# A column gain behind the transposes, and a column stage in written order

## The chip, the cores and the metric

The kernel runs on one core of a Trainium2 chip. The core has a matrix engine (PE), a vector engine (DVE), an activation engine (ACT), a general engine (POOL) and a sync engine (SP), each with its own queue of instructions, and DMA queues that move data between main memory and the on-chip buffers. [...] The metric is the device time of one execution in microseconds. Lower is better.

## The reference

Two layers of a hybrid block over 256 tokens of width 1024, in float32. Each layer normalises x, projects it to 8960 columns, runs four mixers on parts of them (retention A, a gated convolution B, spatial gating C, sliding-window attention D), gates and merges them, and ends in a feed-forward part:

```python
h = rms_norm(x, norm1_g)
z = h @ w_in
za, zb, zc, zd, zg = jnp.split(z, IN_SPLITS, axis=-1)
ya = retention(za, ret_gn_g)
yb = conformer_conv(zb, conv_w, conv_b, conv_ln_g, conv_ln_b)
yc = spatial_gating(zc, gmlp_ln_g, gmlp_ln_b, gmlp_ws, gmlp_bs)
yd = swa_attention(zd, swa_q_g, swa_k_g, swa_sinks, rel_bias)
...
x = x + (mix @ w_out).astype(x.dtype)
h = rms_norm(x, norm2_g)
gt, up = jnp.split(h @ w_ffn_in, 2, axis=-1)
return x + ((jax.nn.silu(gt) * up) @ w_ffn_out).astype(x.dtype)
```

`rms_norm` multiplies x by the inverse root of the mean of its squares and by a gain per column. The change touches how this is computed before the first layer, and the order of the work on `z` in both.

## The kernel before

**Tiles and weights.** The 256 tokens are two tiles of 128 (t = 0, 1). All weights come as *units* of 128 x 2048 values in two halves, in the order of `unit_plan`. A half is fetched (`raw`), rounded by ACT to its high part (`wh`, L119), and DVE subtracts to get its low part (`wl`, L120). Eight buffers of each kind hold four units; six hold raw halves. A 512-column product needs two units. The activations are split in the same way into `hT` high and low (`split`: ACT L176, DVE L178/L180), after PE has transposed them in blocks of 128 x 128 (L169). `mm` makes each product from three matmuls: high x high (L142), high x low weight (L143), low x high (L144). PSUM is four banks `acc`, for the long products, and four banks `mid`, for everything short.

**Opening.** x arrives in two 512-column pieces of tile 0, then four weight halves, then tile 1. ACT and DVE sum the squares, POOL raises to the power -0.5 (`rsqrt`, L186), DVE multiplies x by that factor and by the gain (L239). In the opening the gain comes as two rows of 512, and PE spreads it over 128 partitions with a matmul against a column of ones (L293). PE fills the time before its first work with matmuls on a zeroed tile (`warm_up`, L322). POOL also makes a wide copy (L336) of the table of relative positions. Then come the query columns (units 0 and 1) and the key and value columns (unit 2, 256 wide) of tile 0 and tile 1.

**Column stage (`columns`).** Behind these come eight *chunks*, each of two units over both tiles: convolution a, convolution gate, rotary query, rotary key, retention value, retention gate, gMLP v, gMLP u. The small work of the four mixers is written as generators. `chunk` calls `tick` after each unit, which advances every live generator to its next `yield`; so a `yield` is a step of one unit, about 24 long matmuls.

- `swa_task`: squares, sums and power of queries and keys (L383 to L388, L186), scaled queries and keys (L393, L399), a copy of the values by ACT (`sv`, L405); transposes and their copies (L414, L415); scores by PE (L432), maxima on DVE (L439), exponentials on ACT (L453), their scaling on ACT (L459); transposes of the weights (L469), products with the values (L480).
- `conv_task`: the gate's tanh on ACT (`cvth`, L488), which reads the gate's accumulators, the gate on DVE, transposes to `uT`, then 31 taps on DVE (L510).
- `rot_task`: rotation on DVE (L574 to L582), transposes and copies to `rqk` (L725). `ret_task`: the gate, then scores, products and norm of the retention.

**Who orders the work.** Within a block called `manual_schedule` the named engines issue as the program is written. Before the change that holds for the opening alone, on PE, ACT and DVE. Everywhere else a scheduler orders each engine's instructions. DMAs marked with `keep_in_program_order` stay in written order; before, these are x and the first two units. `take` starts the loading of units two ahead of the one in use (`LOOK`).

## Time and profile before

| What | Value |
|---|---|
| Time, median of 3 runs | 963.24 us (963.23 to 963.3) |
| Profiled execution: its own time | 963.76 us |
| Profiled execution: span, first to last instruction | 961.7 us |
| Mean granted clock of PE | 0.995 |
| Busy: PE, PE weight loads, DVE, ACT, POOL | 952.5, 792.4, 709.7, 507.7, 38.3 us |
| Weight fetches | 320 of 512 KB, median 4.1 us to landing |
| Bytes moved by DMA | 177.00 MB, mean 184 GB/s |

All times below are microseconds from the span's start. A row of the timeline shows its start, how long the group runs, the engine, the line and the tiles (written tile, arrow, read tiles), the count, and in brackets the idle time of the engine just before with what released it. The profiled execution's time is 2.1 us over its span, for what lies before the first and behind the last instruction.

### The profile page before, as it was taken

How to read it: one execution, taken by the hardware profiler on the slowest of the kernel's cores; microseconds unless marked ns; L12 is line 12 of the kernel's file. 1: busy time of each engine (PE TensorE's matmuls, PEld its weight loads, DVE VectorE, ACT ScalarE, POOL GpSimd, SP SyncE). 2: the span in 40 equal slices, each digit the busy share in tenths (PEclk: the TensorE clock that was granted, in tenths of full speed). 3: DMA queues.
4: the chain of work that ended last, by engine and by line, in shares of the span. 5: the costliest groups of instructions: out<-in, count | busy, mean ns of one | idle time of the engine just before them, and what ended most of it. 6: DMA issues, size and time to landing. Idle time of an engine off the chain costs nothing.

```text
span 961.7 us, 12735 instructions
## 1 busy us (share of the span) xinstructions
PE 952.5 (99%) x4686; PEld 792.4 (82%) x4686; DVE 709.7 (74%) x1117; ACT 507.7 (53%) x758; POOL 38.3 (4%) x41
## 2 busy tenths in 40 slices
PE   8999999999999999999999999999999999999998
PEld 5877888888888888888888778888888888888886
DVE  6479999996667766566575699999775677666562
ACT  6298555444635655545464864545445555555550
POOL 1200010000100000000010000200010000000000
PEclk7999999999999999999999999999999999999999
DMA  9764736656546656656557155465655357656621
GB/s 335 209 224 157 254 127 224 193 187 208 177 157 197 219 176 199 195 177 183 166 177 239 66 197 178 151 196 182 202 184 177 113 193 244 194 177 197 196 89 44
DMA packets 50125, 177.00 MB, mean 184 GB/s; under 512 B 5613, under 2 KB 7182, under 8 KB 49936
## 3 DMA queue, kind: packets, MB, share of 16 engines
q1 hardware_dynamic: 49824, 176.07, 56.0%
q8 instruction: 37, 0.61, 0.3%
q14 instruction: 24, 0.20, 0.1%
q10 hardware_dynamic: 240, 0.12, 0.0%
HBM read 174.93 MB, written 1.25 MB: 183 GB/s over the span
## 4 chain that ended last, share of the span: by engine, by line
PE 96%; ACT 1%; DVE 1%; DMA 1%; issue 0%; ACTq 0%; POOL 0%; DVEq 0%; POOLq 0%
PE acc L143 22%; PE acc L144 22%; PE acc L142 22%; PE mid L198 14%; PE mid L201 7%; PE mid L169 3%; PE mid L142 2%; PE mid L143 2%; PE mid L144 2%; ACT sc L453 1%; DMA rel<-rel_bias 1%; PE mid L480 1%; PE mid L469 0%; PE mid L652 0%; DVE wl L120 0%; PE mid L600 0%
## 5 line engine op out<-in xcount | busy, mean ns | idle before, releaser
L120 DVE TENSOR_TENSOR wl<-raw,wh 128x1024 fp32r<-128x1024 f32 x318 | 383.3, 1220 | 129.0 <-ACT wh L119 126.5
L119 ACT CAST wh<-raw 128x1024 fp32r<-128x1024 f32 x318 | 330.8, 1052 | 226.5 <-PE acc L144 129.5
L142 PE MATMUL acc<-wh,hT 128*128 128x512 f32 (+1 forms) x640 | 249.2, 390 | 0.0
L143 PE MATMUL acc<-wl,hT 128*128 128x512 f32 (+1 forms) x640 | 247.1, 386 | 0.2 <-DVE wl L120 0.2
L144 PE MATMUL acc<-wh,hT 128*128 128x512 f32 (+1 forms) x640 | 246.9, 386 | 0.0
L198 PE MATMUL mid<-hT,wh 128*128 128x512 f32 x576 | 203.5, 398 | 0.0
L201 PE MATMUL mid<-hT,wl 128*128 128x256 f32 x576 | 161.7, 281 | 0.0
L142 PEld LDWEIGHTS acc<-wh,hT 128*128 128x128 f32 x640 | 120.8, 189 | 25.0 <-ACT hT L176 1.1
L144 PEld LDWEIGHTS acc<-wh,hT 128*128 128x128 f32 x640 | 120.7, 189 | 24.4 <-DVE hT L180 0.6
L143 PEld LDWEIGHTS acc<-wl,hT 128*128 128x128 f32 x640 | 120.9, 189 | 23.8 <-DVE wl L120 0.8
L198 PEld LDWEIGHTS mid<-hT,wh 128*128 128x128 f32 x576 | 108.1, 188 | 26.2
L142 PE MATMUL acc<-wh,yT 128*128 128x512 f32 x304 | 118.9, 391 | 0.0
L144 PE MATMUL acc<-wh,yT 128*128 128x512 f32 x304 | 118.4, 390 | 0.0
L143 PE MATMUL acc<-wl,yT 128*128 128x512 f32 x304 | 118.4, 389 | 0.0
L201 PEld LDWEIGHTS mid<-hT,wl 128*128 128x128 f32 x576 | 108.8, 189 | 0.4
L510 DVE SCALAR_TENSOR_TENSOR ca<-uT,col,ca 128x256 f32<-128x256 f32 x240 | 101.3, 480 | 3.8 <-ACT ca L504 3.7
L144 PEld LDWEIGHTS acc<-wh,yT 128*128 128x128 f32 x304 | 57.1, 188 | 12.0
L142 PEld LDWEIGHTS acc<-wh,yT 128*128 128x128 f32 x304 | 57.1, 188 | 11.9
L143 PEld LDWEIGHTS acc<-wl,yT 128*128 128x128 f32 x304 | 57.1, 188 | 11.5
L806 ACT ACTIVATE gth<-acc 128x512 f32<-128x512 f32 x32 | 19.1, 597 | 31.0 <-PE acc L144 31.0
L186 POOL TENSOR_TENSOR rs<-rs,nhalf 128x1 f32<-128x1 f32 (+1 forms) x12 | 15.5, 1296 | 373.0 <-DVE rs L525 369.9
L840 DVE TENSOR_TENSOR x<-x,acc 128x512 f32<-128x512 f32 x16 | 10.9, 684 | 24.8 <-PE acc L144 24.8
(161 smaller groups left out, 718.8 us busy)
## 6 DMA issues: line engine op xcount, KB each, us to landing
raw<-wu SPq DMA_DIRECT2D x320, 512.0 KB, 4.1
rows<-rows SPq DMA_DIRECT2D x2, 768.0 KB, 8.7
ng<-norms SPq DMA_DIRECT2D x3, 512.0 KB, 4.2
const<-const SPq DMA_DIRECT2D x1, 1088.0 KB
bias<-rd SPq DMA_DIRECT2D x8, 128.0 KB, 6.0
out<-x SPq DMA_DIRECT2D x4, 256.0 KB, 2.0
x<-x SPq DMA_DIRECT2D x2, 256.0 KB, 3.2
x<-x SPq DMA_DIRECT2D x1, 512.0 KB, 7.9
```

The lines of the kernel that those rows point to most:

```text
L119: nc.scalar.copy(h, src)
L120: nc.vector.tensor_tensor(out=lo, in0=src, in1=h.bitcast(F32), op=ALU.subtract)
L142: nc.tensor.matmul(ps, xh, hs, start=start, stop=False)
L143: nc.tensor.matmul(ps, xh, ls, start=False, stop=False)
L144: nc.tensor.matmul(ps, xl, hs, start=False, stop=stop)
L169: self.nc.tensor.transpose(ps[:, b * P : (b + 1) * P], src[:, b * P : (b + 1) * P], self.ident)
L186: self.nc.gpsimd.tensor_tensor(out=out, in0=v, in1=self.nhalf[:, :n], op=ALU.pow)
L198: nc.tensor.matmul(ps.rearrange("p (s t m) -> p s t m", s=2, t=T), h[:, c : c + P], both, start=start, stop=False)
L201: nc.tensor.matmul(ps[:, : T * P].rearrange("p (t m) -> p t m", t=T), lo[:, c : c + P], self.hT[:, :, 0, k, :], start=False, stop=stop,)
L510: nc.vector.scalar_tensor_tensor(out=self.ca[:, c, :], in0=self.uT[:, c, k : k + T * P], scalar=w[:, c, k : k + 1], in1=self.ca[:, c, :], ...
L806: self.nc.scalar.activation(th[t, n], ps[t], AF.Tanh, scale=0.5)
L840: self.nc.vector.tensor_tensor(out=xs, in0=xs, in1=ps, op=ALU.add)
```

## The change

**Opening.** The gain is no longer spread over partitions. It arrives as eight columns beside the identity matrix (`first`), x is scaled by the root alone (tile halves n = 0 on ACT, n = 1 on DVE), PE transposes it, and DVE then multiplies the transposed half, where a column of gain stands on the partitions, while it copies it out of PSUM to `gT` (`gained`). ACT and DVE split `gT` into high and low. The products are issued half by half of the weights (`half`): per half all high x high, then low x high, then high x low weight. Six weight halves instead of four are fetched ahead of tile 1. The warm-up matmuls number 11, 3, 4 and 3 instead of 7, 3, 1 and 1.

**Column stage.** `columns` of both layers stands in a manual block for PE, ACT, DVE and POOL. The retention's value and gate chunks move ahead of the rotary ones. `swa_task` is spread over more units: tile 0's query transposes one unit earlier, tile 1's scores in two parts, one more unit between softmax and transposes, and one more between these and the products. The first ten units' fetches and all those of constants stay in written order.

The core of the diff:

```diff
-    for c0 in (CONV_A, CONV_G, ROT_Q, ROT_K, RET_V, RET_G, GM_V, GM_U):
+    for c0 in (CONV_A, CONV_G, RET_V, RET_G, ROT_Q, ROT_K, GM_V, GM_U):
...
+            if i < PINNED:
+                self.pin(dma)
...
+    def half(self, ps, act, half, k0, per, n, first=False, last=False):
+        h, lo, _ = half
+        for p, (a, w) in enumerate(((0, h), (1, h), (0, lo))):
+            for i in range(per):
+                self.nc.tensor.matmul(
+                    ps, act[:, a, k0 + i, :], w[:, i * n : (i + 1) * n],
+                    start=first and p == 0 and i == 0, stop=last and p == 2 and i == per - 1,
+                )
...
+        self.first = cp.tile([P, P + 8], F32, name="first")
+        self.ident = self.first[:, :P]
...
+            def scaled(t, ms, hn, n):
+                xs = self.x[t][:, n * 512 : (n + 1) * 512]
+                if n == 0:
+                    nc.scalar.activation(hn[n], xs, AF.Copy, scale=ms[:, 3:4])
+                else:
+                    nc.vector.tensor_scalar(out=hn[n], in0=xs, scalar1=ms[:, 3:4], scalar2=None, op0=ALU.mult)
+
+            def gained(t, hn, n):
+                ps = self.transpose4(hn[n])
+                dst = self.hT[:, t]
+                gT = self.work("gT")
+                v = gT.rearrange("p (k m) -> p k m", k=4)
+                g = self.first[:, P + 4 * n : P + 4 * n + 4].unsqueeze(2).broadcast_to([P, 4, P])
...
+                return (
+                    lambda: nc.vector.tensor_tensor(
+                        out=v, in0=ps.rearrange("p (k m) -> p k m", k=4), in1=g, op=ALU.mult
+                    ),
+                    lambda: nc.scalar.copy(h, v),
+                    lambda: nc.vector.tensor_tensor(out=lo, in0=v, in1=h.bitcast(F32), op=ALU.subtract),
+                )
...
+            warm_up(11)
+            ms, hn = self.norm_sums(0, True)
+            nc.vector.memset(warm[:, W : W + P], 0.0)
+            warm_up(3, c=W)
+            nc.gpsimd.tensor_copy(
+                out=wide, in_=relhot[:, 0:8].unsqueeze(1).broadcast_to([REL + 1, COPIES, 8])
+            )
             for n in range(2):
-                nc.tensor.matmul(gps[n], self.ones, grow[n], start=True, stop=True)
-            self.warm_up(3)
-            hn = self.norm(0, raw=gps)
+                scaled(0, ms, hn, n)
+            h0, h1 = (self.hT[:, t] for t in range(T))
+            a0, a1 = (gained(0, hn, n) for n in range(2))
+            warm_up(4)
+            high(0)
+            for f in (a0[0], a1[0], a0[1]):
+                f()
+            high(1)
+            a1[1]()
+            for i in range(2, 6):
+                high(i)
+            a0[2]()
+            low(0)
+            low(1)
+            a1[2]()
+            low(2)
+            low(3)
+            low(4)
+            ms, hn = self.norm_sums(1)
+            low(5)
+            z = [(self.abank(), self.abank())]
+            for i in range(4):
+                self.half(z[0][0], h0, w[i], 2 * i, 2, 512, i == 0, i == 3)
...
+                self.half(z[0][1][:, :256], h0, w[4 + i], 4 * i, 4, 256, i == 0, i == 1)
...
+                scaled(1, ms, hn, n)
+            b0, b1 = (gained(1, hn, n) for n in range(2))
+            warm_up(3)
+            for f in (b0[0], b0[1], b1[0], b1[1], b0[2], b1[2]):
+                f()
...
     def swa_task(self, t, psq, pskv):
         qk = self.swa_qk(t, psq, pskv)
         yield
-        yield
+        for _ in range(t):
+            yield
         self.swa_qkT(t, *qk)
         yield
         yield
-        sc = self.swa_soft(t)
+        sc = self.b8.tile([P, 8, P * (t + 1)], F32, tag="b8", name="sc")
+        mx = self.small("mx", 8)
+        for j0 in (0, 2):
+            self.swa_scores(t, sc, mx, j0)
+            if j0 == 0 and t == 1:
+                yield
+        self.swa_soft(sc, mx)
+        yield
         yield
         yield
         pT = self.swa_pT(t, sc)
+        yield
         yield
         self.emit_y(3, t, self.swa_pv(t, pT), 1.0)
...
-    def ret_task(self, pg):
-        for t in range(T):
-            self.ret_gate(t, pg[t])
+    def ret_task(self):
+        yield
         yield
...
+            if ready and t == 0:
                 self.layer_constants(0)
...
+        self.ahead(self.pos + 2)
...
+        pa = self.chunk(hT)
...
-        pa = self.chunk(hT)
...
+        pg = self.chunk(hT)
...
-        pg = self.chunk(hT)
         tasks[1] = self.spawn(self.conv_task(pa, pg))
-        pq = self.chunk(hT)
-        self.rqk = self.b8.tile([P, 2, 4, T * P], F32, tag="b8", name="rqk")
...
-        pk = self.chunk(hT)
-        tk = self.spawn(self.rot_task(pk, 1))
         pv = self.chunk(hT)
...
-        tasks[0] = self.spawn(self.ret_task(pg))
+        for t in range(T):
+            self.ret_gate(t, pg[t])
+        pq = self.chunk(hT)
+        self.rqk = self.b8.tile([P, 2, 4, T * P], F32, tag="b8", name="rqk")
+        self.spawn(self.rot_task(pq, 0))
+        pk = self.chunk(hT)
+        self.spawn(self.rot_task(pk, 1))
+        tasks[0] = self.spawn(self.ret_task())
...
         for l in range(L):
-            hT, need = self.columns(l, h0, h1)
+            with self.tc.manual_schedule(engines=ORDERED):
+                hT, need = self.columns(l, h0, h1, ready if l == 0 else None)
...
+ORDERED = {
+    mybir.EngineType.PE, mybir.EngineType.Activation, mybir.EngineType.DVE, mybir.EngineType.Pool
+}
...
-LOOK = 2
+PINNED = 10
...
+        "first": np.concatenate([ident, i["norm1_g"][0].reshape(8, P).T], 1),
```

Three places show what moves. Each fence gives one engine's queue, before and then after.

POOL in the opening, from its first instructions for the kernel on (`ms` holds the sum of squares and the root of tile 0, `wide` the table's copy; ISA belongs to the instruction behind it). Before:

```order
L265 MEMSET ones 1x128
L266 MEMSET nhalf 128x96
L268 MEMSET uT 128x4x30
L328 MEMSET rel 1x8
L336 COPY wide<-rel 33x128
L186 ISA
L186 TENSOR_TENSOR ms<-ms,nhalf 128x1
```

After:

```order
L282 MEMSET nhalf 128x96
L284 MEMSET uT 128x4x30
L198 ISA
L198 TENSOR_TENSOR ms<-ms,nhalf 128x1
L347 COPY wide<-relhot 33x128
```

The power of tile 0 stood behind the copy of the table and now stands ahead of it.

ACT behind the key and value columns of the first layer (`sv` the values, `swsq` and `jk` the squares of queries and keys, `wh` high halves of weights, two to a unit). Before:

```order
L383 ACTIVATE swsq_307<-acc_243 128x512
L384 ACTIVATE jk_308<-acc_244 128x128
L119 CAST wh_229<-raw_231 128x1024
L119 CAST wh_233<-raw_235 128x1024
L405 COPY sv_241<-acc_244 128x128
L383 ACTIVATE swsq_378<-acc_328 128x512
L384 ACTIVATE jk_379<-acc_329 128x128
L405 COPY sv_241<-acc_329 128x128
```

After:

```order
L439 ACTIVATE swsq_346<-acc_200 128x512
L440 ACTIVATE jk_347<-acc_201 128x128
L461 COPY sv_344<-acc_201 128x128
L439 ACTIVATE swsq_367<-acc_289 128x512
L440 ACTIVATE jk_368<-acc_290 128x128
L461 COPY sv_344<-acc_290 128x128
L122 CAST wh_382<-raw_384 128x1024
L122 CAST wh_386<-raw_388 128x1024
L122 CAST wh_403<-raw_405 128x1024
L122 CAST wh_407<-raw_409 128x1024
```

Casts stood between the squares and the copy of the values; now both tiles' copies stand ahead of the next casts.

ACT around the softmax of tile 0, first layer (`sc` the scores, `den` their sums, `es` the sink's term, `cvth` the tanh of the convolution's gate). Before:

```order
L119 CAST wh<-raw 128x1024
L453 ACTIVATE sc,den<-sc,nm 128x128 x2
L119 CAST wh<-raw 128x1024
L453 ACTIVATE sc,den<-sc,nm 128x128
L119 CAST wh<-raw 128x1024
L453 ACTIVATE sc,den<-sc,nm 128x128 x3
L459 ACTIVATE sc<-sc,den 128x128 x5
L119 CAST wh<-raw 128x1024
L459 ACTIVATE sc<-sc,den 128x128 x2
L119 CAST wh<-raw 128x1024
L459 ACTIVATE sc<-sc,den 128x128
L488 ACTIVATE cvth<-acc 128x512
```

After:

```order
L470 COPY swqT<-mid 128x512 x2
L122 CAST wh<-raw 128x1024 x4
L506 ACTIVATE es<-es 128x8
L509 ACTIVATE sc,den<-sc,nm 128x128 x8
L515 ACTIVATE sc<-sc,den 128x128 x8
L544 ACTIVATE cvth<-acc 128x512 x2
L122 CAST wh<-raw 128x1024 x4
```

The casts that lay between single exponentials and scalings now stand ahead of and behind the whole softmax, and both tanh stand behind it.

More of the change, by code (lines that the diff above doesn't have):

```diff
@@ L216, in fold, with norm_sums @@
         self.nc.vector.tensor_tensor(out=out, in0=main, in1=out, op=ALU.add)
-    def norm(self, t, raw=None):
+    def norm_sums(self, t, dve=False):
         nc = self.nc
         x = self.x[t]
-        g = raw or [self.ng[:, n * 512 : (n + 1) * 512] for n in range(2)]
         ms = self.small("ms")
-        hn = [self.work("hn") for _ in range(2)]
+        junk = [self.work("hn") for _ in range(2)]
         for n in range(2):
             xs = x[:, n * 512 : (n + 1) * 512]
-            if raw and n == 1:
+            if dve and n == 1:
                 nc.vector.tensor_tensor_reduce(
-                    out=hn[n], in0=xs, in1=xs, scale=1.0 / D, scalar=0.0,
+                    out=junk[n], in0=xs, in1=xs, scale=1.0 / D, scalar=0.0,
                     op0=ALU.mult, op1=ALU.add, accum_out=ms[:, n : n + 1],
@@ L236, in norm, with norm_scale @@
         self.rsqrt(ms[:, 3:4], ms[:, 2:3])
+        return ms, junk
+    def norm_scale(self, t, sums, g):
+        ms, hn = sums
         for n in range(2):
-            s = slice(n * 512, (n + 1) * 512)
-            nc.vector.scalar_tensor_tensor(
-                out=hn[n], in0=x[:, s], scalar=ms[:, 3:4], in1=g[n], op0=ALU.mult, op1=ALU.mult
-            )
-        if raw:
-            return hn
+            self.nc.vector.scalar_tensor_tensor(
+                out=hn[n], in0=self.x[t][:, n * 512 : (n + 1) * 512], scalar=ms[:, 3:4], in1=g[n],
+                op0=ALU.mult, op1=ALU.mult,
+            )
+        return hn
+    def norm(self, t):
+        hn = self.norm_scale(t, self.norm_sums(t), [self.ng[:, n * 512 : (n + 1) * 512] for n in range(2)])
         def late():
@@ L270, in opening @@
     def opening(self):
-        nc, a, pin = self.nc, self.a, self.tc.keep_in_program_order
+        nc, a, pin = self.nc, self.a, self.pin
         self.setup()
+        nc.scalar.dma_start(out=self.first, in_=a["first"])
         for n in range(2):
@@ L275, in opening @@
             pin(nc.sync.dma_start(out=self.x[0][:, c], in_=a["x"][0:P, c]))
-        grow = []
-        for n in range(2):
-            grow.append(self.wk.tile([1, W], F32, tag="wk", name="grow"))
-            nc.scalar.dma_start(out=grow[n], in_=a["norms"][0, 0:1, n * 512 : (n + 1) * 512])
-        nc.scalar.dma_start(out=self.ident, in_=a["ident"])
-        rel, hot = self.bias_inputs()
-        first = self.fetch(0, True) + self.fetch(1, True)
-        self.next_load = 2
-        pin(nc.sync.dma_start(out=self.x[1], in_=a["x"][P : 2 * P]))
@@ L316, in opening @@
-        self.bias_rows(rel, hot)
-        return h0
-    def warm_up(self, n):
-        ps = self.bank()
-        for _ in range(n):
-            self.nc.tensor.matmul(ps, self.warm[:, :P], self.warm, start=True, stop=True)
-    def bias_inputs(self):
-        nc, cp, a = self.nc, self.cp, self.a
-        rel = cp.tile([REL + 1, 8], F32, name="rel")
-        hot = self.wk.tile([REL + 1, 384], F32, tag="wk", name="hot")
-        nc.gpsimd.memset(rel[REL : REL + 1, :], 1.0)
-        nc.scalar.dma_start(out=rel[0:REL, :], in_=a["rel_bias"])
-        nc.scalar.dma_start(out=hot, in_=a["hot"])
-        return rel, hot
@@ L333, in bias_rows @@
-    def bias_rows(self, rel, hot):
-        nc = self.nc
-        wide = self.sm.tile([REL + 1, COPIES, 8], F32, tag="kn", name="wide", bufs=2)
-        nc.gpsimd.tensor_copy(out=wide, in_=rel.unsqueeze(1).broadcast_to([REL + 1, COPIES, 8]))
-        ps = self.bank()
-        nc.tensor.matmul(ps[:, :384], wide.rearrange("p c h -> p (c h)"), hot, start=True, stop=True)
-        r = self.work("r8")
-        nc.scalar.copy(r[:, :384], ps[:, :384])
+        relhot = self.wk.tile([REL + 1, 8 + 384], F32, tag="wk", name="relhot")
@@ L350, in constants @@
             )
-            nc.sync.dma_start(out=self.bias[COPIES * i : COPIES * (i + 1)], in_=skew)
-        self.const = cp.tile([P, NCONST], F32, name="const")
-        nc.sync.dma_start(out=self.const, in_=a["const"])
+            self.pin(self.nc.sync.dma_start(out=self.bias[COPIES * i : COPIES * (i + 1)], in_=skew))
+    def constants(self):
+        self.const = self.cp.tile([P, NCONST], F32, name="const")
+        self.pin(self.nc.sync.dma_start(out=self.const, in_=self.a["const"]))
     def layer_constants(self, l):
@@ L969, in run @@
     def run(self):
-        self.pos = 0
         self.tasks = []
         self.mT = {}
-        h0 = self.opening()
-        h1 = self.norm(1)
+        h0, h1, ready = self.opening()
+        for i in range(3):
+            self.units.pop(i)
         for l in range(L):
-            hT, need = self.columns(l, h0, h1)
+            with self.tc.manual_schedule(engines=ORDERED):
+                hT, need = self.columns(l, h0, h1, ready if l == 0 else None)
             self.ng = self.load_norm(l, 1)
@@ L1062 @@
         "wsT": np.ascontiguousarray(i["gmlp_ws"].transpose(0, 3, 1, 2)),
-        "rel_bias": np.ascontiguousarray(i["rel_bias"]),
-        "const": const, "hot": hot, "ident": ident,
+        "relhot": np.concatenate([np.concatenate([i["rel_bias"], np.ones((1, 8), f32)], 0), hot], 1),
+        "const": const,
+        "first": np.concatenate([ident, i["norm1_g"][0].reshape(8, P).T], 1),
     }
```

160 lines of the change are left out of this document (84 added, 76 removed).

## Prediction

> **What bounds the kernel now.** I read the page's busy table first, then the waits of the matrix engine (PE), then the opening and the attention stages in the timeline.
>
> ```profile
> PE 952.5 (99%) x4686; PEld 792.4 (82%) x4686; DVE 709.7 (74%) x1117; ACT 507.7 (53%) x758; POOL 38.3 (4%) x41
> ```
>
> PE is busy for 952.5 of 961.7 us: the kernel is a fixed amount of matmul work plus what PE loses. A change that leaves the matmuls alone can only win or lose idle and half-clock time. These PE rows (start, duration, and in brackets the idle time before with its releaser) bracket the opening:
>
> ```profile
> 1.17 2.98 PE L322 MATMUL mid<-warm 128*128 128x512 bf16 x7 [1.17 <-DVE warm L289]
> 4.08 1.98 PE L293 MATMUL acc<-grow,ones 1*128 1x512 f32 x4
> 5.99 0.82 PE L322 MATMUL mid<-warm 128*128 128x512 bf16 x3
> 9.49 1.12 PE L169 MATMUL mid<-ident,hn 128*128 128x128 f32 x4 [2.67 <-DVE hn L239]
> 13.82 0.79 PE L142 MATMUL acc<-wh,hT 128*128 128x512 f32 x1
> 17.90 0.39 PE L143 MATMUL acc<-wl,hT 128*128 128x512 f32 x1
> 18.13 0.40 PE L144 MATMUL acc<-wh,hT 128*128 128x512 f32 x1
> 30.77 0.28 PE L143 MATMUL acc<-wl,hT 128*128 128x256 f32 x1
> 30.89 0.28 PE L144 MATMUL acc<-wh,hT 128*128 128x256 f32 x1
> 33.16 0.40 PE L142 MATMUL acc<-wh,hT 128*128 128x512 f32 x1
> ```
>
> Real work starts at 13.82; the query, key and value columns of both token tiles end at 33.16, where the first convolution chunk starts. Starts lie 0.23 us apart at 512 columns and 0.12 at 256, so those columns need 48 x 0.23 + 48 x 0.12, some 16.6 us: half of the first 33 us is loss. Further on, PE's larger losses are in the attention stages of both layers:
>
> ```profile
> 46.87 1.34 PE L432 MATMUL mid<-skT,swqT 64*128 64x256 f32 x8 [0.27 <-DVE mx L439]
> 50.12 0.50 PE L143 MATMUL acc<-wl,hT 128*128 128x512 f32 x1 [0.18 <-DVE wl L120]
> 529.78 2.20 PE L432 MATMUL mid<-skT,swqT 64*128 64x256 f32 x16 [0.62 <-DVE mx L439]
> 545.39 0.73 PE L469 MATMUL mid<-ident,sc 128*128 128x128 f32 x2 [0.48 <-ACT sc L459]
> ```
>
> These idles add to 1.55. Matmuls that start late without an idle record bring both stages to an estimated 2.7. That is all that the attention part of the change can remove.
>
> **Part 1: the opening.** Removed: two gain matmuls (row 4.08), two copies of the gain out of PSUM, the gain's fetch. Added: per token tile, two multiplies of a transposed half by a gain column on DVE. Moved: POOL's power ahead of its copy, tile 1's transposes behind all of tile 0's columns, and x's second tile behind six weight halves instead of four.
>
> ```profile
> 4.49 0.69 DVE L227 CUSTOM_DVE_ANT_0 hn<-x 128x512 f32<-128x512 f32 x1 [3.37 <-DMA x<-x]
> 5.30 0.21 DVE L233 TENSOR_SCALAR ms<-ms 128x1 f32<-128x1 f32 x1
> 7.76 0.28 POOL L336 COPY wide<-rel 33x128 f32<-33x128 f32 x1 [6.43 <-DMA rel<-rel_bias]
> 8.09 0.56 POOL L186 TENSOR_TENSOR ms<-ms,nhalf 128x1 f32<-128x1 f32 x1
> 8.68 1.41 DVE L239 SCALAR_TENSOR_TENSOR hn<-x,ms,acc 128x512 f32<-128x512 f32 x2 [3.17 <-POOL ms L186]
> 15.47 2.35 DVE L120 TENSOR_TENSOR wl<-raw,wh 128x1024 fp32r<-128x1024 f32 x2
> 16.95 2.00 ACT L119 CAST wh<-raw 128x1024 fp32r<-128x1024 f32 x2
> ```
>
> The sums are ready at 5.51, but the power runs at 8.09, behind a copy that waits for a transfer. Moved ahead it ends near 6.15. The two scalings then run side by side on ACT and DVE (0.7 each, half of row 8.68) and end near 6.85; eight transposes at 0.11 follow. DVE gets the first product at 7.6 and then works without pause: two gains and two low parts at 0.65 (a half of row 8.68's kind), six low halves at 1.17 and a 0.2 sum: 7.6 + 2.6 + 7.0 + 0.2 = 17.4. ACT's six casts at 1.0 fit beside it, and so does x's second tile if the transfers keep their rate. PE follows DVE and ends tile 0 at 17.9; tile 1 needs 0.9 for transposes and, behind the first four, one gain and one cast, so it starts near 19.8 and takes 8.3. The first chunk starts at **28.2 instead of 33.16: a gain of 4.9**. The multiply by a column has no row; its nearest are the 0.69 and 0.7 above, so 0.6 to 0.8 each. Bounds of the term: 5.9 if each link is a few tenths shorter, 1.7 if the clock stays low (second rival).
>
> **Part 2: the columns in written order.** The matmuls stay. What changes is who stands in front of whom on ACT and DVE, priced by these rows:
>
> ```profile
> 504.27 0.68 DVE L386 TENSOR_REDUCE swms<-swsq 128x8 f32<-128x512 f32 x1
> 507.13 0.28 DVE L387 TENSOR_REDUCE swms<-jk 128x2 f32<-128x128 f32 x1
> 508.79 1.96 POOL L186 TENSOR_TENSOR swrs<-swms,nhalf 128x10 f32<-128x10 f32 x1 [9.01 <-DVE swms L388]
> 511.71 0.27 ACT L405 COPY sv<-acc 128x128 f32<-128x128 f32 x1 [5.25 <-DVE kn L399]
> 517.09 1.07 ACT L414 COPY swqT<-mid 128x512 f32<-128x512 f32 x2
> 46.10 0.29 DVE L439 CUSTOM_DVE_ANT_0 sc<-mid,bias 128x128 f32<-128x128 f32 x1 [0.38 <-PE mid L432]
> 48.31 0.40 ACT L453 ACTIVATE sc<-sc,nm 128x128 f32<-128x128 f32 x1 [1.53 <-DVE nm L447]
> 532.71 0.40 ACT L453 ACTIVATE sc<-sc,nm 128x128 f32<-128x128 f32 x1 [3.08 <-DVE nm L447]
> 536.53 2.45 ACT L459 ACTIVATE sc<-sc,den 128x128 f32<-128x128 f32 x8 [0.53 <-DVE den L457]
> 525.38 0.60 ACT L488 ACTIVATE cvth<-acc 128x512 f32<-128x512 f32 x1 [1.62 <-PE acc L144]
> ```
>
> *(a) ACT waits in its copy of the values (sv).* Row 511.71 shows that this copy starts only after DVE has scaled the keys, 2.9 us after the power began (508.79). Today casts stand ahead of it; in written order six casts stand behind it. Layer 0: DVE's two low halves of unit 3 end at 24.2; reductions 1.1 and 2.9 bring tile 0's copy to an end at 28.4; tile 1's squares, reductions and power take until 33.0, its copy until 33.25, the cast of the next half 34.3, its low part 35.5. PE wants that low part at 28.2 + 5.4 (24 matmuls of a unit) + 0.5 (transposes) + 0.2 = 34.4, so it waits **1.1**. In layer 1 tile 0's part is long done, and the same sum from the end of the value columns gives **0.3**. Bounds: 0 (the chain starts a microsecond earlier) and 2.9 (a whole power).
>
> *(b) The convolution's tanh behind a softmax.* The third chunk's first accumulator is the one that the gate's tanh (cvth) reads, and on ACT cvth now stands behind all of tile 0's softmax. Counted from tile 1's query transposes: copy 1.2; one cast 1.05 and four low halves at 1.17 on DVE end at 7.0; from the first maximum to the first exponential 2.2 (46.10 to 48.31); exponentials and sum 3.8 (532.71 to 536.53); scalings 2.4; tanh 0.6: about 16.0 with hand-overs. PE arrives after two units (10.9), transposes 0.5 and scores 2.3, at 13.7. It waits **2.3, in each layer**. What is queued behind cvth is four casts and tile 1's softmax, so DVE's convolution taps start late too. Bounds: 1 and 3.5.
>
> *(c) The rotary products behind the taps.* These two rows, first and last of one rotation, and one of taps:
>
> ```profile
> 74.13 0.68 DVE L574 TENSOR_TENSOR r<-acc,const 128x512 f32<-128x512 f32 x1
> 75.51 0.69 DVE L582 TENSOR_TENSOR r<-r,r 128x512 f32<-128x512 f32 x1
> 78.50 4.57 DVE L510 SCALAR_TENSOR_TENSOR ca<-uT,col,ca 128x256 f32<-128x256 f32 x11 [2.29 <-ACT ca L504]
> ```
>
> From the third chunk's start DVE is held by ACT (casts, tile 1's softmax, four drains, four tap starts, two value copies, one cast) until 22.1. Then come four low halves 4.7, eight taps 3.3, a low part of the output, the gates 2.4, four low halves 4.7, four taps 1.7; a wait for ACT's cast of tile 1's output until 40.7; a low part 0.6, four taps 1.7 and two rotations at 2.0: 47. PE reaches the second tile's transposes at 45.9 (seven units and 7.8 of transposes and small matmuls) and waits **1.0, in each layer**. Bounds: 0 and 2.5.
>
> **The sum.** Gain 4.9 + 2.7 = 7.6; new waits 1.1 + 0.3 + 2 x 2.3 + 2 x 1.0 = 8.0; net +0.4 on the profiled execution's 963.76, that is 964.2. That execution lies 0.5 above the median of 963.24, so I forecast **963.6: no change**. About 0.2%, or 1.9 us, is what a measurement of this kernel tells from none. SP's and POOL's reorderings I cost at nothing: after the opening weights land well ahead, and POOL is busy for 38.3 us of the span. If that cover went, a late weight half would cost one transfer.
>
> **The rivals.** *The gain stays (faster).* If ACT and DVE are quicker by the lower bounds of (a) to (c), waits come to 0 + 2 x 1 + 0, with 1.5 for small ones: 3.5. The time is 963.24 - 7.6 + 3.5 = 959.1. For it: ACT is busy for only 53%. Against: every link of (b) has a row. Chance 0.36.
>
> *The clock does not hold (slower).* These windows are 3.41 us long; the columns are PE, PEld, DVE, ACT and POOL busy (instructions), then the granted clock, DMA share and GB/s:
>
> ```profile
> 0.42:3.83 3.41, 2.66 (x7) 0.89 (x7) 0.27 (x1) 0.99 (x1) 0.56 (x5) 1.00 0.55 166
> 3.83:7.24 3.41, 2.98 (x9) 0.87 (x7) 0.92 (x3) 1.01 (x3) 0.00 (x0) 1.00 0.95 283
> 7.24:10.66 3.42, 1.17 (x5) 1.08 (x6) 1.41 (x2) 1.12 (x3) 0.84 (x2) 0.50 0.97 398
> 10.66:14.07 3.41, 3.41 (x9) 1.55 (x8) 2.16 (x3) 3.41 (x6) 0.00 (x0) 0.50 1.06 427
> 14.07:17.49 3.42, 3.42 (x9) 2.65 (x10) 3.42 (x4) 3.42 (x8) 1.56 (x2) 0.50 1.00 418
> ```
>
> The clock fell at 7.24 after a window in which PE was busy for 2.98, but 1.9 of that were the one-row gain matmuls; it did not rise at 14.07 after a window full of transposes and a 33-row matmul; it rose at 17.49 after one full of 128-row matmuls. [...] The changed kernel drops the gain matmuls and runs 11 + 3 full-size warm-ups: about 1.7 us of full-size work in the second window against 0.9 before. If that is still too little, PE stays at half clock from 7.24 to 14.07; the matmuls of tile 0 that fall before it then take twice as long, tile 0 ends at 21.1, the first chunk starts at 31.4, and the time is 963.6 + 3.2 = 966.8. Chance 0.17.
>
> [...]
>
> *Wait (b) drops the clock (slower).* [...] One window at half clock costs 1.7 a layer: 963.6 + 1.7 or + 3.4, so 965.3 to 967.0. Chance 0.10.
>
> *The order is not as written.* On DVE it holds up to the last unit but one of the columns; after that rows are mixed as before, so the sum is not touched.
>
> **How the numbers follow.** Forecast 0.37, gain stays 0.36, clock 0.17, clock by the wait 0.10. Its own range, from the bounds of (a) to (c), is 961.3 to 965.2. For 8 in 10 it must reach the rivals, on the faster side with the opening's upper bound (5.9 instead of 4.9): 958.1 to 967.0. Faster 0.36, within 0.2% 0.37, slower 0.27.
>
> **What would show it.** The first convolution chunk starting near 28 with the clock column at 1.00 from 3.83 on proves part 1. An idle time of PE at the first matmul of the third chunk, released by ACT's cvth, in both layers, proves (b); its absence, or one under 1 us, makes the forecast too slow. Idle time before a matmul with wl in the first chunk's second half is (a), and before the rotary transposes, released by DVE, is (c). A clock column of 0.50 behind 7.24, or behind cvth's wait, is a slower rival.

## The result and the profile after

The changed kernel takes **995.36 us** (median of 5 runs, 995.05 to 996.68) against 963.24 before: 1.0335 times as long, 95% interval 1.0324 to 1.0347. Its profiled execution took 996.61 with a span of 994.6 and a mean granted clock of 0.985; against the profiled execution of before that is +32.85. The forecast was 963.6, the range ended at 967.0: both were wrong.

The busy table of the changed kernel (busy time, share of the span, instructions):

```profile
PE 962.6 (97%) x4691; PEld 795.1 (80%) x4691; DVE 715.5 (72%) x1120; ACT 505.7 (51%) x758; POOL 34.9 (4%) x39
```

PE is busy for 10.1 us longer with five more matmuls, so some of its work ran at a lower clock, and it is idle for 32.0 instead of 9.2. Both parts add to the 32.9. The waits of PE in the changed kernel (line that waits, engine and line waited for: us in total, times, longest):

```profile
PE mid L708 <- DVE gv L700: 7.0, 2, 3.5
PE acc L145 <- ACT cvth L544: 4.4, 2, 2.5
PE mid L181 <- DVE ry L678: 4.1, 4, 1.5
PE acc L145 <- DVE gu L687: 4.0, 2, 2.0
PE mid L708 <- DVE nb L588: 2.6, 2, 1.3
PE mid L181 <- DVE r L638: 1.9, 2, 1.0
...
PE acc L146 <- DVE wl L123: 0.9, 2, 0.6
```

Three of these lines are the waits of the forecast: cvth is (b), r is (c), wl is (a). The four with gv, ry, gu and nb, 17.7 us together, are in none of its terms. They lie at the end of each layer's column stage. Where the time is lost shows by the start of the first low-half matmul of a chunk in both traces:

| Landmark | Before | After | Difference |
|---|---|---|---|
| Layer 0, first convolution chunk | 33.40 | 31.03 | -2.37 |
| Layer 0, first gates chunk | 140.82 | 143.38 | +2.56 |
| Layer 0, second gates chunk | 155.27 | 169.06 | +13.79 |
| Layer 0, first project chunk | 277.70 | 293.92 | +16.22 |
| Layer 1, first gates chunk | 612.49 | 631.46 | +18.97 |
| Layer 1, first project chunk | 749.36 | 782.05 | +32.69 |

So the ways up to the first gates chunk (with the opening in layer 0, from the first layer's project chunk in layer 1) cost 2.6 and 2.75, and the stretch from there to the project chunk 13.7 in each layer: 27.4 of 32.85. The largest step, 11.23, lies between the rows of the first and the second gates chunk in layer 0, first before and then after:

```profile
140.82 0.39 PE L143 MATMUL acc<-wl,hT 128*128 128x512 f32 x1
...
155.27 0.39 PE L143 MATMUL acc<-wl,hT 128*128 128x512 f32 x1
```

```profile
143.38 0.39 PE L146 MATMUL acc<-wl,hT 128*128 128x512 f32 x1
...
169.06 0.63 PE L146 MATMUL acc<-wl,hT 128*128 128x512 f32 x1
```

PE in this stretch of layer 0 (rows as in the timelines of the prediction), and its windows (columns as there):

```profile
157.67 1.15 PE L708 MATMUL mid<-gv,ws 128*128 128x128 f32 x8 [3.48 <-DVE gv L700]
160.12 2.04 PE L708 MATMUL mid<-gv,ws 128*128 128x128 f32 x8 [1.30 <-DVE nb L588]
162.69 1.11 PE L181 MATMUL mid<-first,ry 128*128 128x128 f32 x4 [0.52 <-DVE ry L678]
165.34 1.11 PE L181 MATMUL mid<-first,ry 128*128 128x128 f32 x4 [1.54 <-DVE ry L678]
168.46 0.79 PE L145 MATMUL acc<-wh,hT 128*128 128x512 f32 x1 [2.01 <-DVE gu L687]
```

```profile
154.00:157.42 3.42, 0.19 (x1) 0.00 (x0) 3.42 (x4) 1.04 (x1) 0.68 (x1) 1.00 0.88 299
157.42:160.83 3.41, 1.85 (x11) 1.70 (x12) 3.41 (x10) 0.74 (x3) 0.00 (x0) 0.68 0.72 265
160.83:164.24 3.41, 2.45 (x11) 1.76 (x9) 3.41 (x11) 2.26 (x8) 0.00 (x0) 0.50 0.02 5
164.24:167.66 3.42, 1.11 (x4) 0.71 (x4) 2.78 (x6) 2.15 (x6) 0.00 (x0) 0.50 0.00 0
```

PE waits 8.9 us in five pieces, and its clock falls to a half. The trace records it at 0.50 from 158.65 to 172.30; PE is busy for 8.3 us of that, so some 4.1 go to the clock, and the two make 13.0 of the 13.7. DVE is full in all but the last window. What it does is in its two largest groups between 142.6 and 165.2 (busy time, mean ns | idle time before), where it is busy for 22.4 of 22.6. Below them stand the first rows of that stretch and the last:

```profile
L123 DVE TENSOR_TENSOR wl<-raw,wh 128x1024 fp32r<-128x1024 f32 x8 | 9.6, 1206 | 0.2 <-ACT wh L122 0.2
L566 DVE SCALAR_TENSOR_TENSOR ca<-uT,col,ca 128x256 f32<-128x256 f32 x17 | 7.4, 475 | 0.0
```

```profile
142.82 1.21 DVE L123 TENSOR_TENSOR wl<-raw,wh 128x1024 fp32r<-128x1024 f32 x1
143.95 0.17 DVE L578 BATCH_NORM_AGGREGATE bmv<-bst 128x2 f32<-128x6 f32 x1
144.04 0.26 DVE L577 BATCH_NORM_STATS2 bst<-mid 128x6 f32<-128x128 f32 x1
...
165.21 0.68 DVE L685 SCALAR_TENSOR_TENSOR gus<-gus,acc 128x512 f32<-128x512 f32 x1
```

Eight low halves (9.6) and sixteen tap instructions (6.9; the seventeenth in the view is one of the block's own, which ends as the stretch begins) stand between the rows that the written block ends with: the retention's statistics (L577, L578), the normalised gMLP values (gv), the retention's output (nb, ry) and the first step of the last gelu (gus). The low halves belong to units of the gate stage, and the sixteen taps to later steps of the convolution: both are written behind the block. The statistics come one at a time: behind each of the first four stands a low half of 1.2, behind most of the others a tap of 0.46. In the kernel before, the gelu's first step ran right behind the last column chunk, at 140.80:

```profile
140.80 0.68 DVE L629 SCALAR_TENSOR_TENSOR gus<-gus,acc 128x512 f32<-128x512 f32 x1
```

Here it runs at 165.21. It is written behind nb and ry, and on ACT the square that it needs is written behind ry, which waits for nb:

```profile
160.09 1.50 ACT L593 ACTIVATE ry<-mid,nb,rs 128x128 f32<-128x128 f32 x4 [4.81 <-DVE nb L588]
...
164.13 0.61 ACT L684 ACTIVATE gus<-acc 128x512 f32<-128x512 f32 x1
```

Only gu, the last step of that gelu, frees the accumulators that the second gates chunk writes: PE's last wait, at 168.46.

### The profile page after: what moved, and what is told of

It is laid out like the page before. It is cut to its first block, busy times and chain, and to the rows that moved or that the text cites. A ratio compares the mean times of both kernels' runs of the same rounds, so it can differ in the third digit from the quotient of the medians.

```text
span 994.6 us, 12708 instructions
## 1 busy us (share of the span) xinstructions
PE 962.6 (97%) x4691; PEld 795.1 (80%) x4691; DVE 715.5 (72%) x1120; ACT 505.7 (51%) x758; POOL 34.9 (4%) x39
## 4 chain that ended last, share of the span: by engine, by line
PE 90%; DVE 5%; ACT 2%; issue 1%; POOL 1%; DMA 0%; SPq 0%; POOLq 0%; ACTq 0%; DVEq 0%
PE acc L145 20%; PE acc L146 20%; PE acc L147 20%; PE mid L210 14%; PE mid L213 7%; PE mid L181 2%; PE mid L145 1%; PE mid L147 1%; PE mid L146 1%; DVE ca L566 1%; PE acc L153 1%; ACT sc L509 1%; DVE wl L123 1%; POOL swrs L198 1%; PE mid L536 1%
## 5 line engine op out<-in xcount | busy, mean ns | idle before, releaser
L123 DVE TENSOR_TENSOR wl<-raw,wh 128x1024 fp32r<-128x1024 f32 x314 | 377.1, 1223 | 130.3 <-ACT wh L122 127.6
L122 ACT CAST wh<-raw 128x1024 fp32r<-128x1024 f32 x314 | 322.7, 1052 | 212.4 <-PE acc L147 112.1
L145 PE MATMUL acc<-wh,hT 128*128 128x512 f32 (+1 forms) x608 | 241.1, 396 | 8.4 <-ACT cvth L544 4.4
L146 PE MATMUL acc<-wl,hT 128*128 128x512 f32 (+1 forms) x608 | 237.6, 391 | 0.9 <-DVE wl L123 0.9
L147 PE MATMUL acc<-wh,hT 128*128 128x512 f32 (+1 forms) x608 | 237.5, 391 | 0.0
L145 PEld LDWEIGHTS acc<-wh,hT 128*128 128x128 f32 x608 | 115.4, 190 | 34.4 <-ACT cvth L544 5.2
L147 PEld LDWEIGHTS acc<-wh,hT 128*128 128x128 f32 x608 | 115.2, 190 | 24.7 <-DVE hT L192 0.6
L146 PEld LDWEIGHTS acc<-wl,hT 128*128 128x128 f32 x608 | 115.6, 190 | 24.2 <-DVE wl L123 1.5
```

The lines of the kernel that those rows point to most:

```text
L122: nc.scalar.copy(h, src)
L123: nc.vector.tensor_tensor(out=lo, in0=src, in1=h.bitcast(F32), op=ALU.subtract)
L145: nc.tensor.matmul(ps, xh, hs, start=start, stop=False)
L146: nc.tensor.matmul(ps, xh, ls, start=False, stop=False)
L147: nc.tensor.matmul(ps, xl, hs, start=False, stop=stop)
```

## The experiments

Every kernel here computes the whole reference. Times are medians; "before" on the same chips lay between 963.1 and 963.5. "End step" is what the way from the first to the second gates chunk of layer 0 takes more than in the kernel before: 11.23 in the changed kernel.

### Whose order costs the time

The columns of both layers outside the written block, the rest of the change kept:

```diff
-            with self.tc.manual_schedule(engines=ORDERED):
-                hT, need = self.columns(l, h0, h1, ready if l == 0 else None)
+            hT, need = self.columns(l, h0, h1, ready if l == 0 else None)
```

> The opening, the new chunk order and the spread of the attention stay; inside the column stage no engine is held to the written order, the scheduler orders all of them. Theory A (the written order costs the 32 us): both layers lose their 16.3, and only the 2.4 of the opening remain, so 961 (959 to 963), with the idle time of PE ahead of the second gate chunk below 1. Rival B (the new chunk order and the spread put too much DVE work at the end of the stage, whoever orders it): 985 or more.

Measured: 962.67, ratio 0.9997 (0.9987 to 1.0006). The end step is +0.03. The whole loss comes with the written order; the new opening, the new chunk order, the spread attention and the fetches in written order make no measurable difference together.

Then one engine at a time was taken out of the list, DVE and ACT first:

```diff
-            with self.tc.manual_schedule(engines=ORDERED):
+            with self.tc.manual_schedule(engines=ORDERED - {mybir.EngineType.DVE}):
```

> As the changed kernel, but DVE's instructions of the column stage are ordered by the scheduler; PE, ACT and POOL stay as written. If DVE's own written order is what makes the last rows late, the loss falls by more than half: 980 or less. If ACT's written order is (tile 1's softmax ahead of the taps' start, the retention's norm ahead of the squares of gMLP u), it stays: 988 to 996.

> As the changed kernel, but ACT's instructions of the column stage are ordered by the scheduler; PE, DVE and POOL stay as written. If ACT's written order is at fault, the taps start earlier and the squares of gMLP u no longer stand behind the retention's norm: 975 or less, and the 2.5 us wait for the convolution's tanh goes too. If DVE's is, it stays: 988 to 996.

> As the changed kernel, but PE's instructions of the column stage are ordered by the scheduler; ACT, DVE and POOL stay as written. If PE merely stands behind its own written rows (spatial gating ahead of the gates' products), it has other work and the step between the first two gate chunks falls from 11.2 to under 5: 975 to 985. If DVE's late rows hold the accumulators that PE needs next, PE has no other work: 990 to 998.

| Left to the scheduler | Time | Ratio (95%) | End step |
|---|---|---|---|
| DVE | 972.48 | 1.0098 (1.0082 to 1.0115) | +0.03 |
| ACT | 1000.97 | 1.0390 (1.0364 to 1.0415) | +11.73 |
| PE | 991.58 | 1.0296 (1.0279 to 1.0312) | +11.23 |

Of the three, only DVE's order carries the end step. ACT free came out above both of its expected ranges. With DVE free, PE's wait for cvth is most of what remains, and it is longer than in the changed kernel:

```profile
PE acc L145 <- ACT cvth L544: 7.3, 2, 5.3
```

### Why DVE is late: too much work, or work in the wrong place

Two theories were left. One: DVE carries a backlog out of the attention (low halves, two softmaxes and taps), and the written rows come late because of it. Two: DVE has time enough, but low halves and taps stand ahead of rows that PE needs. The backlog was taken away by planning 8 us of taps into later units, behind the block:

```diff
-TAP_PLAN = (1,) * 8 + (0, 1) * 4 + (1,) * 4 + (2,) * 7
+TAP_PLAN = (0,) * 5 + (1,) * 3 + (0, 1) * 2 + (1,) * 5 + (2,) * 10
```

> The plan of the taps moves five of the 31 taps (20 instructions of 0.4 us, 8 us of DVE) from the column stage into the gate stage; all else as in the changed kernel. Theory A (DVE enters the end of the stage with a backlog, and its written rows there come late by it): the step of 13.6 us at the end of each column stage falls by 6 or more, 970 to 984. Rival B (not the amount of work but the weight halves of the gates that are mixed in ahead of the last written rows): less than 3 a layer, 989 to 996.

Measured: 991.81, ratio 1.0304 (1.0281 to 1.0327), end step +9.79. DVE carries no backlog into the end of the stage: it waits 0.7 for ACT at 129.63 and at 132.75 here, and in the changed kernel, too, at 131.62 and at 134.73. Yet eight low halves and thirteen taps stand between the last rows, and the waits stay. So the backlog falls as the cause; the moved taps stand behind the block, where they can be put between the rows as well.

A second edit moved only the retention's normalisation one unit later, so that the last gelu is written ahead of it:

```diff
         st = [self.ret_out(t) for t in range(T)]
         yield
+        yield
         ys = [self.ret_norm(t, *st[t]) for t in range(T)]
```

> One more step ahead of the retention's norm, so that on ACT the squares of gMLP u (which free the accumulators of the second gate chunk) stand ahead of the norm's scalings. All else as in the changed kernel. If ACT's queue at the end of the stage is the wait, the step of 11.2 us between first and second gate chunk falls to 3 to 5 in each layer: 979 to 983. If DVE's backlog is, the squares wait no longer but the products on DVE still do: 990 to 996.

Measured: 988.19, ratio 1.0260 (1.0245 to 1.0276), end step +5.68, between the two expected ranges. PE no longer waits for gu, so the accumulators come free in time, but it now waits longer for the values ahead of them:

```profile
PE mid L708 <- DVE gv L700: 10.3, 4, 4.4
```

Which row is written last decides what waits, not whether something waits. So the last chunk was left out of the block: the written order ends ahead of the chunk that feeds the gMLP's u, and all that is emitted with it (the same DVE rows) goes to the scheduler:

```diff
         tv = self.spawn(self.gv_task(pv))
+        self.guard.__exit__(None, None, None)
         pu = self.chunk(hT)
...
```

> The written order ends ahead of the last chunk (gMLP u) instead of behind it; all else as in the changed kernel. Theory A (backlog of DVE, made by the written order earlier in the stage): the backlog is the same at that point, half of the step at the end stays, 978 to 990. Rival B (the last written rows, with scheduled rows mixed in between): the step at the end goes, as when DVE is free, and 16 x 2 becomes 3 x 2: 966 to 972.

Measured: 968.24 (967.29 to 972.33), ratio 1.0065 (1.0042 to 1.0088), end step -0.49. DVE's low halves in the corresponding stretch (139.88 to 151.86) and the rows that were late:

```profile
L123 DVE TENSOR_TENSOR wl<-raw,wh 128x1024 fp32r<-128x1024 f32 x3 | 3.6, 1218 | 0.0
```

```profile
146.18 0.16 DVE L588 SCALAR_TENSOR_TENSOR nb<-bmv,rs 128x4 f32<-128x4 f32 x1
...
151.87 0.68 DVE L685 SCALAR_TENSOR_TENSOR gus<-gus,acc 128x512 f32<-128x512 f32 x1
```

Three low halves and no tap instead of eight and sixteen, 16.5 us of work down to 3.6, and both rows come some 13 us earlier. PE does not wait there any more.

If the unordered low halves are what gets in between, it should help to write the loads and splits of the next units inside the block, behind its last rows:

```diff
         tasks[2] = self.spawn(self.gm_task(pu))
+        self.ahead(self.pos + 4)
```

> The loading of the gates' second pair of units is written inside the block, behind the last rows, so that no low half of a weight can be mixed in ahead of them; taps still can (26 instead of 16 now stand among them). DVE's work between the first statistics of the retention and the first product of gMLP u falls from 16.3 us (8 halves and 16 taps) to 10.7. If these rows are the delay, the step at the end of the stage falls from 13.6 to about 8 in each layer: 981 to 988. If the amount does not matter, it stays at 993 to 996.

Measured: 988.49, ratio 1.0257 (1.0241 to 1.0273), end step +7.46. No low half stands among the rows any more, but 24 taps do, where there were 16 (26 were expected). Something else that is unordered fills the place; 3.8 of 11.2 is won.

### What remains: the forecast's waits (b) and (c)

With the last chunk free, wait (b) is the largest left, and (c) stands at 1.9 as in the changed kernel:

```profile
PE acc L145 <- ACT cvth L544: 4.6, 2, 2.6
```

For (b), still with the last chunk free, tile 0's scalings by the softmax's sum were moved two units later, so that the convolution's tanh stands ahead of them on ACT:

```diff
...
-        self.swa_soft(sc, mx)
-        yield
-        yield
+        den = self.swa_soft(sc, mx)
+        if t == 0:
+            yield
+            yield
+        self.swa_rescale(sc, den)
+        if t:
+            yield
+            yield
```

> From the kernel whose block ends ahead of the last chunk (968.2): tile 0's eight scalings of the softmax (2.45 us on ACT) are written two steps later, so that the two tanh of the convolution's gate stand ahead of them. The wait ahead of the third chunk (2.6 and 2.0 in the two layers) should fall to 0.3 or less, and the half clock behind it in layer 0 should go: 962 to 964. If ACT is late for another reason, wait and time stay: 967 to 969.

Measured: 963.12, ratio 0.9996 (0.9987 to 1.0005). The wait is gone from the list, and no window of that stretch shows a clock under 1.00. From the convolution's second chunk to the fourth chunk, layer 0 takes 4.0 us less than in the changed kernel: the 2.5 of the wait, and 1.5 that the lower clock behind it had cost.

For (c), the rotary transposes of the queries go one unit later on top of that:

```diff
         rs = [self.rotary(t, ps[t]) for t in range(T)]
         yield
+        if i == 0:
+            yield
```

> From the kernel with the tanh ahead of the scalings (963.1): the rotated queries are transposed one unit later, so that PE need not wait for DVE's rotation. The waits of 1.0 ahead of these transposes, one in each layer, should go: 961 (960.5 to 961.8), 0.2 to 0.3% under the kernel before. If DVE is late by more than one unit, or another wait takes the place (the retention's scores behind the rotated keys), 962.5 to 963.5.

Measured: **961.95** (961.75 to 962.12, 11 runs), ratio 0.9984 (0.9975 to 0.9993): 1.2 of the 1.9 is won. This kernel is 0.16% under the kernel before, with an interval clear of 1; the difference is small all the same, for three of the 15 executions of the kernel before on that chip took 961.9 to 962.2. Of PE's waits in the column stages, (a) and this are left:

```profile
PE acc L146 <- DVE wl L123: 0.9, 2, 0.6
...
PE mid L181 <- DVE r L642: 0.3, 2, 0.2
```

### The opening by itself

The new opening with the column stage of before (chunk order, attention, left to the scheduler), the fetches of ten units and of the constants kept in written order:

```diff
-    for c0 in (CONV_A, CONV_G, RET_V, RET_G, ROT_Q, ROT_K, GM_V, GM_U):
+    for c0 in (CONV_A, CONV_G, ROT_Q, ROT_K, RET_V, RET_G, GM_V, GM_U):
...
-            with self.tc.manual_schedule(engines=ORDERED):
-                hT, need = self.columns(l, h0, h1, ready if l == 0 else None)
+            hT, need = self.columns(l, h0, h1, ready if l == 0 else None)
...
```

> The new opening with the column stage of the kernel before: its chunk order, its attention steps, ordered by the scheduler. The opening is worth 2.4 by the start of the first chunk (30.8 against 33.2). If it is kept to the end: 960.8. If the attention stage of layer 0 takes it back as in the run with all engines free (DVE comes to it later by as much): 962.5 to 963.3, no change.

Measured: 972.16, ratio 1.0094 (1.0078 to 1.0110), far above both expected times. PE's two largest waits:

```profile
PE acc L145 <- ACT cvth L544: 3.9, 1, 3.9
PE acc L145 <- ACT wh L122: 3.1, 1, 3.1
```

The second is new. The cast waits for a weight half that is queued on SP behind the relative bias, its eight copies and the constants (issued from 22.97 on, the eight copies alone until 30.8). So the same kernel with three units in written order and the constants' transfers free:

```diff
-PINNED = 10
+PINNED = 3
...
-        self.pin(self.nc.sync.dma_start(out=self.const, in_=self.a["const"]))
+        self.nc.sync.dma_start(out=self.const, in_=self.a["const"])
...
```

> The new opening with the column stage of the kernel before, and without the written order of the fetches behind the first three units, so that the transfers are queued as in the kernel before. If the late weights (a wait of 3.1 for a cast whose half landed late) and what they pushed were the cause of the 972 of the opening with written fetches, that goes and the opening's 2.4 show: 960 to 961.5. If the opening itself collides with the attention of layer 0, 963 or more.

Measured: 965.73, ratio 1.0028 (1.0017 to 1.0040). 6.4 us come back, yet the kernel is slower than before, although its first chunk starts 1.1 earlier (32.08), and would start 2.1 earlier without a wait of 1.05 right ahead of it. What PE waits for:

```profile
PE acc L145 <- ACT cvth L544: 1.9, 1, 1.9
PE acc L145 <- DVE swqn L449: 1.0, 1, 1.0
```

The earlier chunk meets an accumulator that DVE's scaling of the queries has not freed yet, and then a tanh behind the softmax. With the new chunk order and the spread attention, and also scheduled, the first experiment is 3.1 faster, which is level with the kernel before. (It keeps the written order of the fetches, so the two kernels differ in that as well.)

The last run takes the first experiment and warms up with seven matmuls instead of eleven, to test the rival of the clock:

```diff
-            warm_up(11)
+            warm_up(7)
```

> From the kernel with all engines free in the column stage (962.7): 7 instead of 11 matmuls of warm-up ahead of the first sum of squares, 7 x 0.4 = 2.8 us of PE instead of 4.45. [...]

Measured: 963.15, ratio 0.9999 (0.9990 to 1.0008), 0.5 slower than with eleven, though on another chip. In the profiled executions, too, the first low-half matmul of the first chunk starts 0.5 later (31.56 against 31.05). A window and the matmuls at its end of this kernel, then the matmuls of the changed one:

```profile
3.83:7.25 3.42, 1.74 (x5) 0.28 (x3) 1.47 (x5) 1.35 (x4) 0.79 (x2) 1.00 1.02 359
...
6.01 1.46 PE L306 MATMUL mid<-warm 128*128 128x512 bf16 x3 [1.68 <-DVE warm L345]
7.39 1.97 PE L181 MATMUL mid<-first,hn 128*128 128x128 f32 x8
```

```profile
6.12 0.82 PE L306 MATMUL mid<-warm 128*128 128x512 bf16 x3 [0.49 <-DVE warm L345]
7.49 1.09 PE L181 MATMUL mid<-first,hn 128*128 128x128 f32 x8 [0.56 <-ACT hn L324]
```

The matmuls take 1.8 times as long for a short while. The column's 1.00 says nothing here: in the changed kernel, too, it shows 1.00 ahead of that trace's first record of the clock, at 5.05, while the warm-ups start 0.43 apart. By the rows the clock is back soon after: the first four products, at 10.13, take 1.35 here and 1.46 in the changed kernel. So four warm-ups are worth half a microsecond here, not the 3.2 of the rival. The times on record for this run were 964 to 966, or no change; it came out nearer to no change.

## Why the prediction was wrong, step by step

**The step that failed** is its fourth rival, which closes with "after that rows are mixed as before, so the sum is not touched". The order does end there, as the forecast said. But "as before" is not what the scheduler then does: in the kernel before, it chose among all rows and put the gelu's first step at 140.80. Here the block's rows keep their order among themselves, and rows from behind the block are put between them, so the last rows of a chain in written order each wait behind other work. The sum followed DVE up to the rotary products and stopped there; the stretch behind them cost 27.4. That it is DVE's order at the end of the block, and neither PE's order nor the work ahead of that end, is shown by four runs: DVE free and the last chunk free take the step away, later taps and PE free leave most of it. That the delay is the work mixed in is read from the trace: it fills 16.5 of the 22.4 us for which DVE is busy there. The run that was to keep that work out took only the low halves out, and won 3.8.

**Opening (4.9 forecast, 2.4 measured).** DVE is nearly as worked out: the low halves of tile 0 end at 17.79 (forecast: products done at 17.4, low halves included), and one multiply by a column takes 0.65, as the sum had it.

```profile
8.18 1.29 DVE L336 TENSOR_TENSOR gT<-mid,first 128x512 f32<-128x512 f32 x2 [0.98 <-PE mid L181]
16.57 1.22 DVE L319 TENSOR_TENSOR wl<-raw,wh 128x1024 fp32r<-128x1024 f32 x1
```

PE's rows there are these:

```profile
9.58 1.46 PE L153 MATMUL acc<-wh,hT 128*128 128x512 f32 x4
...
12.10 0.91 PE L376 MATMUL mid<-relhot,wide 33*128 33x384 f32 x2
...
20.03 1.04 PE L181 MATMUL mid<-first,hn 128*128 128x128 f32 x8
...
22.07 1.46 PE L153 MATMUL acc<-wh,hT 128*128 128x512 f32 x4 [0.35 <-ACT hT L339]
...
30.80 0.40 PE L145 MATMUL acc<-wh,hT 128*128 128x512 f32 x1
```

What failed is "PE follows DVE and ends tile 0 at 17.9". PE starts tile 0 at 9.58, with 8.3 of its own to do, the bias products of 0.9 put in between, a wait of 0.4 for a low half, and first products that start more than 0.3 apart instead of 0.23: it ends at 20.0 and was the bound itself. Tile 1 then went as worked out (2.0 of hand-over for 1.9, 8.7 for 8.3). Both starts, 33.16 and 30.80, are those of one execution; the kernel before took 961.8 to 965.1 in its 22 executions on one chip, with mean granted clocks of 0.994 to 1.000, so the gain need not be 2.4 in each.

**Attention's own waits (2.7 forecast).** They are gone from the list of waits, but little time came with them. In the fastest kernel, where little else is lost but (a), the way from the first convolution chunk to the first project chunk of layer 0 costs +0.26 against before. Together with the 0.6 of (a) that leaves some 0.4 for the attention of layer 0, where half of the 2.7, 1.35, was put in.

**(a) 1.1 and 0.3 forecast; 0.62 and 0.3 measured.** **(c) 1.0 each; 0.96 each.** (a) came by its chain: ACT's copy of tile 1's values waited 3.97 for DVE's scaled keys and ended at 35.6 instead of 33.25, and PE's first chunk was as much later. (c) came at the place and behind the engine that were named.

**(b) 2.3 each forecast; 2.47 and 1.95 measured**, at the place and behind the engine that were named. The rival "wait (b) drops the clock" came true in layer 0 alone:

```profile
59.69 0.79 PE L145 MATMUL acc<-wh,hT 128*128 128x512 f32 x1 [2.47 <-ACT cvth L544]
549.30 0.50 PE L145 MATMUL acc<-wh,hT 128*128 128x512 f32 x1 [1.95 <-ACT cvth L544]
```

```profile
56.26:59.67 3.41, 0.96 (x8) 0.51 (x8) 1.79 (x10) 2.96 (x10) 0.00 (x0) 1.00 0.17 71
59.67:63.08 3.41, 3.39 (x8) 2.71 (x9) 3.28 (x4) 3.41 (x5) 0.00 (x0) 0.50 0.00 0
547.77:551.18 3.41, 1.88 (x8) 1.56 (x9) 2.84 (x11) 3.41 (x8) 0.00 (x0) 1.00 0.00 0
```

These windows are laid where this trace records that the clock changes (59.66 and 63.08, then on in steps of 3.41). In layer 0 nearly all of the wait fell into one window and left PE busy for 0.96 of it; the clock was at 0.50 for the window behind it, which cost 1.5 (1.7 was the rival's price). In layer 1 the window kept 1.88, and the clock stayed at 1.00. Where the steps lie differs from trace to trace: whole steps back from the recorded changes, the first one behind the span's start lies at 1.64 in the changed kernel and at 0.42 in the kernel before, and with one and the same opening the eleven warm-up matmuls took from 4.05 (opening alone) to 4.75 us (norm later). So I take it for luck, an estimate, that the rival came true in one layer and not in both or none.

**Sum up to the first gates chunk.** Forecast +0.4, measured 2.56 + 2.75 = 5.3: opening 2.5 short, attention about 2 short, 1.5 of clock, less 0.7 that (a) and (b) were too dear. These make 5.3, where the difference is 4.9; the 0.4 left over is not accounted for. The forecast of no change would have been wrong without the missed stretch, too, by 4.9. The forecast's own range, 961.3 to 965.2, is not what the bounds of (a) to (c) give: it is 0.2% either way of 963.24, while the upper bounds (2.9, twice 3.5, twice 2.5) add to 14.9 and, with the gain of 7.6, put the time at 970.5.

**"The clock does not hold"** in the opening: it held, here and in seven other profiled kernels with eleven warm-ups, where the eight transposes behind them take 1.09 as they do here (1.97 with seven warm-ups). No run shows the rival's 3.2; with seven warm-ups 0.5 was lost. In the window in which it fell to 0.50 before, it stands at 1.00 now:

```profile
7.24:10.66 3.42, 3.04 (x16) 1.81 (x16) 2.39 (x4) 2.89 (x5) 0.00 (x0) 1.00 1.02 412
```

**"SP's and POOL's reorderings I cost at nothing":** SP's cost nothing that shows together with the new column stage, for the first experiment keeps them and is level with the kernel before. Without that stage the opening by itself waited 3.1 for one weight half, and freeing the transfers was worth 6.4. No run tries POOL's by itself.

**What stays open.** Why the scheduler puts rows from behind the block between the block's last rows, and why taps take the low halves' place, isn't settled: the runs show that it does and what it costs. A block that reaches over the gates, so that nothing unordered follows, would show what the written order costs without the mixing; no run here has one.

## What to carry to other kernels

Follow a written order past its end: count, on the fullest engine, what unordered work may be put between its last rows and who waits for the last of them, above all for the row that frees an accumulator. A written order should end where its rows have slack, here one chunk earlier, which took 27 us of loss away. And an opening that ends earlier is worth only what the next stage can take up: with the column stage of before, the new opening made a slower kernel, and with the new one in scheduled order a kernel level with the one before.

## What the runs showed of the hardware

The trace of the changed kernel records the granted clock at 1.00 from 5.05 and at 0.50 from 59.66 to 63.08, from 158.65 to 172.30 and from 646.76 to 660.41; that of the kernel before has it at 1.00 from 3.83 and at 0.50 from 7.24 to 17.49. Within each of the two traces these times lie whole steps of 3.41 us apart. PE's busy time in the step ahead of each fall, and in the step of the changed kernel that holds most of wait (b) of layer 1:

| Kernel | Step | PE busy | Clock behind it |
|---|---|---|---|
| Changed | 56.26 to 59.67 | 0.96 | 0.50 |
| Changed | 155.24 to 158.65 | 0.98 | 0.50 |
| Changed | 643.34 to 646.76 | 1.01 | 0.50 |
| Changed | 547.77 to 551.18 | 1.88 | 1.00 |
| Before | 3.83 to 7.24 | 2.98, of which 1.9 one-row matmuls | 0.50 |

What decides between the two clocks, these runs do not show: the last row has the longest busy time and the clock fell all the same. Idle pieces of about 2 us went both ways: the wait of 2.47 ended in a step at 0.50 (layer 0), the one of 1.95 in a step at 1.00 with 1.00 behind it (layer 1). The kernel with the last chunk free shows the price: 967.3 in three executions with a mean granted clock of 1.000, 972.2 and 972.3 in two with 0.995.

Ahead of the first record the clock column shows 1.00 in both profiles (0.42 to 3.83), so there the durations have to be read. In the changed kernel, whose first record is at 5.05, the warm-up matmuls start 0.43 apart up to 5.0 and about 0.22 apart behind it. With seven warm-ups the column shows 1.00 from 3.83 to 10.66, yet three warm-up matmuls at 6.01 took 1.46 instead of 0.82, and eight transposes at 7.39 took 1.97 instead of 1.09.
